# Four edits to a two-layer diffusion step on one core: weight splits held back at sublayer boundaries, modulation of a block on one engine, four-block high and low tiles, and more modulation blocks on TensorE

## Chip, cores and metric

One core of a Trainium2 chip. The metric is device time in microseconds of one execution, as the median of several runs. Beside it stands one execution that was taken with the profiler; all rows below are from that one.

## What is computed

Two layers of a backbone (D = 2048) over 256 tokens: 128 context tokens and 128 noisy ones (below: two groups of 128). Each layer has a mixing and a channel sublayer, each with a norm and a modulation ahead and a norm and a gate behind:

```
def _layer(x, cvec, p, attend):
    shift1, scale1, gate1, shift2, scale2, gate2 = _modulation(cvec, p['w_mod'], p['b_mod'])
    h = _rmsnorm(x, p['g_pre_mix']) * (1 + scale1) + shift1
    au, av, q, k, v, ga, gb = jnp.split(h @ p['w_in'], SPLITS, axis=-1)
    ya = _spatial_gating(au, av, p['sgu_ln_g'], p['sgu_ln_b'], p['sgu_w'], p['sgu_b'])
    yb, extra = attend(_heads(q), _heads(k), _heads(v))
    merged = jax.nn.sigmoid(ga) * (ya @ p['w_pa']) + jax.nn.sigmoid(gb) * (_merge_heads(yb) @ p['w_pb'])
    x = x + gate1 * _rmsnorm(merged @ p['w_out'], p['g_post_mix'])
    h = _rmsnorm(x, p['g_pre_ffn']) * (1 + scale2) + shift2
    f = jnp.square(jax.nn.relu(h @ p['w_ff1'])) @ p['w_ff2']
    x = x + gate2 * _rmsnorm(f, p['g_post_ffn'])
    return x, extra
```

`_modulation` is `silu(cvec) @ w_mod + b_mod` with a 2048 x 12288 matrix per layer and one vector per group of tokens. All weights are float32.

## The kernel before, in words

**Products.** A weight comes in tiles of 128x1024 float32 (512 KB), 928 of them; a tile is a *job* (class `Job`, L51), and eight jobs with the same outputs are a *column* of 512 outputs. `split` (L297) cuts a raw tile into a high and a low part: ACT copies it rounded (`wh`), DVE subtracts (`wl`). Activations stand as high and low parts too, in tiles for two blocks of 128 rows (`pair`, four blocks in the change). `mm_half` (L304) issues for each job and group of tokens high x high, low x high and high x low (L318 to L320 with tokens as output rows, L327 to L329 with features as rows).

**Order.** The body writes a list `items` of jobs and calls, and a loop (L1046 to L1087) goes through it once; the order of the program's text is the order on each engine. Before each item `advance` (L1009) issues what may run ahead: loads of modulation blocks (`mraw`) and of raw tiles (`raw`), through `fetch` (L1004) on SP's queue, and splits while fewer than `P["cap"]` split tiles wait for use.

**Modulation.** The two modulation matrices are 48 *quads* of eight blocks of 512 KB. `MOD_ON_PE` (L45), made from `PE_QUADS` (L38), says where a quad runs: on DVE by `mod_dot` (L180), two SCALAR_TENSOR_TENSOR per block, or on PE by `mod_mm` (L225, matmuls at L234), closed for a quad by `mod_fin` (L209, transposes at L216). Between jobs the loop puts in a block when a pace allows it; for DVE only if its load is under a limit, for PE two at a time. `need(n)` (L859) is the due time: it runs blocks until n quads are done, whatever they wait for. `ENDS` (L37) holds n for the four sublayers' ends.

**A boundary.** At a sublayer's end, x gets the gated, normed output, is normed again, scaled and shifted, and turned so that it can be the next product's stationary side. This is `chain` (L760), one for each group: the norm's factor, four updates of x on DVE and four Squares on ACT, the second norm's factor, and then for each of four tiles of 512 columns the scaling (DVE, tile `s`), four transposes on PE (L803), the modulation (even blocks DVE, odd blocks ACT), the high copy (ACT) and the low subtraction (DVE). PE's cover for it are two columns that `lay_halves` (L839) lays out by halves: the last column of the old sublayer first for group 0, then for group 1, then the first column of the next in the same way; a half job is six matmuls. `step` pumps the chain of group 0 from the middle of the last column on, that of group 1 from the middle of the next, at the positions of `CHAIN_AT`. `cap(HELD)`, eight items ahead of the last column, lets eight splits be made ahead. There are three such boundaries (mixing to channel, channel to the second layer's mixing, mixing to channel), and one end without a next column. At the second one x is also spilled to HBM (L778).

```
        first = (lambda a: lambda p: (lambda: step(0, p - 8, *a)()))(args)
        lay_halves(seq[-1], first)
...
                step(0, p + 8, *a)()
                step(1, p, *a)()
...
        lay_halves(seqs[i][0][0], second)
```

All functions that the edits touch:

Of the kernel before, what the change touches and what calls it, by code (L numbers as in the profile page):

```python
# [23 lines left out]
HELD = 8  # L24
# [12 lines left out]
ENDS = [20, 34, 44, 48]  # L37
PE_QUADS = set(range(11)) | {18, 19}  # L38
# [8 lines left out]
CHAIN_AT = (0, 1, 3, 4, 5, 6, 7, 8, 9, 10, 11, 12)  # L47
# [41 lines left out]
def body(tc, io):  # L89
# [153 lines left out]
    def pair():  # L243
        return u4(F32R).rearrange("p (k h t) -> p k h t", k=2, h=2)

    def hi_lo(t, hl):
        act(hl[:, :, 0, :], t, AF.Copy)
        tt(hl[:, :, 1, :], t, f(hl[:, :, 0, :]), op=OP.subtract)
# [22 lines left out]
    def h_part(todo, tiles, r2, l, ma, mb, c, steps, flush):  # L271
        def finish():
            t, hl, s, u = todo.pop(0)
            tt(hl[:, u, 1, :], t[:, s, :], f(hl[:, u, 0, :]), op=OP.subtract)

        t, hls = tiles
        for b0, n in steps:
# [26 lines left out]
    def mm_half(job, gs=(0, 1)):  # L304
# [5 lines left out]
        for j in range(2):  # L310
            kt = 2 * job.kh + j
            hl = G.rhs[kt // 2][:, kt % 2]
            first, last = kt % n == 0, kt % n == n - 1
            if G.tok:
                for g in gs:
                    o = G.ps[:, 512 * g:512 * g + 512]
                    hh, lo = (hl[:, h, 128 * g:128 * g + 128] for h in range(2))
# [3 lines left out]
            else:  # L321
                hh, lo = hl[:, 0, :], hl[:, 1, :]
# [11 lines left out]
    def mixing(l, hs):  # L334
# [31 lines left out]
        def sgu():  # L366
# [22 lines left out]
            ya = [pair() for _ in range(4)]  # L389
            for k in range(4):  # L390
# [21 lines left out]
        S["yav"] = []  # L412
        S["ybv"] = []
# [51 lines left out]
        def attention():  # L465
            yb = [pair() for _ in range(4)]
            for t in range(4):
# [50 lines left out]
                hi, lo = yb[t][:, :, 0, 128:], yb[t][:, :, 1, 128:]  # L518
# [3 lines left out]
            for t in range(2):  # L522
# [79 lines left out]
        def merge(t, ma):  # L602
# [3 lines left out]
            for e in range(2):  # L606
# [5 lines left out]
                hl = pair()  # L612
                act(hl[:, :, 0, :], v4(o, 2), AF.Copy, scale=0.5)
                yield
                yield
                dve.scalar_tensor_tensor(hl[:, :, 1, :], v4(o, 2), 0.5, f(hl[:, :, 0, :]), op0=OP.mult, op1=OP.subtract)
                mg.append(hl)

        def merged(n):
            def go():  # L620
                while len(mg) < n:
                    pump(bg)
            return go
# [69 lines left out]
    def out_stats(Y, src, o, g):  # L693
        act(dump, src, AF.Square, accum_out=Y["st"][g][:, o:o + 1])
        y = Y["y"][o][:, g, :]
        tt(y, src, y, op=OP.mult)

    def ffn(l, hs):
# [4 lines left out]
        def post_ff1(hid):  # L703
            def post(ps):
# [3 lines left out]
                for h in range(2):  # L708
                    hid.append(pair())
                    hi_lo(v4(t)[:, 2 * h:2 * h + 2, :], hid[-1])  # L710
            return post

        def post_ff1_rows(hid):
            def turn(t, g):
# [4 lines left out]
                w = slice(128 * g, 128 * g + 128)  # L719
                for e in range(2):  # L720
                    act(hid[e][:, :, 0, w], v4(o)[:, 2 * e:2 * e + 2, :], AF.Copy)
                yield
                for e in range(2):
                    tt(hid[e][:, :, 1, w], v4(o)[:, 2 * e:2 * e + 2, :], f(hid[e][:, :, 0, w]), op=OP.subtract)

            def post(ps, gs):
                for g in gs:
                    if g == 0:
                        hid.extend([pair(), pair()])
# [451 lines left out]
```

## Time and profile before

| | |
|---|---|
| median of 3 runs | 2870.31 us (2866.93 to 2874.01) |
| profiled execution | 2869.48 us, span 2867.7 us |
| mean granted clock of PE in it | 0.988 |
| busy: PE, PEld, DVE, ACT | 96%, 83%, 74%, 45% of the span |
| HBM | 713.42 MB read, 6.37 MB written, 251 GB/s over the span |

PE is TensorE's matmuls, PEld its weight loads (beside the matmuls), DVE VectorE, ACT ScalarE, SP SyncE, which issues the loads. The busy share is a mean over the whole span. A wait is the idle time ahead of an instruction together with what ended it. The granted clock is a share of full speed. The profiled execution is 0.8 us below the median.

### The profile page before, as it was taken

The numbers are of one execution on the slowest core, as the hardware profiler recorded it, in microseconds if no ns is written. First come the engines' busy times: TensorE is split into PE (matmuls) and PEld (weight loads), VectorE is DVE, ScalarE is ACT, GpSimd is POOL, SyncE is SP. The second block draws the span as 40 slices with busy tenths as digits, with TensorE's granted clock in tenths as the row PEclk, the third lists the DMA queues.
The fourth block names the chain that finished last, engine by engine and source line by source line (L and its number), as shares of the span: only waits on it lengthen the run. The fifth ranks groups of instructions, "written<-read, shape, count | busy, mean of one in ns | idle before, by whom it ended". The sixth has DMA issues, their size and how long they took to land.

```text
span 2867.7 us, 41916 instructions
## 1 busy us (share of the span) xinstructions
PE 2761.1 (96%) x16366; PEld 2386.6 (83%) x16366; DVE 2114.4 (74%) x2782; ACT 1288.7 (45%) x1654; POOL 0.7 (0%) x6
## 2 busy tenths in 40 slices
PE   7999999997799999999989999999979999999998
PEld 5788778884698989989868997888869899898997
DVE  4665878885579898898866888888865555656555
ACT  4344555442544444444454445544445444444443
POOL 0000000000000000000000000000000000000000
PEclk9999999998999999999999999999999999999999
DMA  9978867787468778787856677677845665756653
GB/s 383 363 261 311 288 227 270 264 314 274 148 232 297 271 270 302 258 302 273 299 183 252 234 261 264 238 273 270 312 145 206 206 223 195 249 191 213 218 201 140
DMA packets 204823, 722.57 MB, mean 252 GB/s; under 512 B 22992, under 2 KB 25680, under 8 KB 204624
## 3 DMA queue, kind: packets, MB, share of 16 engines
q1 hardware_dynamic: 204624, 719.89, 70.3%
q8 instruction: 128, 2.10, 0.3%
q14 instruction: 71, 0.58, 0.1%
HBM read 713.42 MB, written 6.37 MB: 251 GB/s over the span
## 4 chain that ended last, share of the span: by engine, by line
PE 91%; DVE 3%; ACT 3%; DMA 1%; issue 1%; SPq 0%; DVEq 0%; ACTq 0%
PE mm L318 18%; PE mm L320 18%; PE mm L319 18%; PE mm L327 11%; PE mm L328 11%; PE mm L329 11%; PE aux L234 2%; ACT wh L76 1%; DVE u L76 1%; DVE wl L76 1%; DMA mraw<-wm 1%; DVE s L76 1%; ACT s L76 1%; ACT u L76 1%; PE aux L803 0%
## 5 line engine op out<-in xcount | busy, mean ns | idle before, releaser
L76 DVE TENSOR_TENSOR wl<-raw,wh 128x1024 fp32r<-128x1024 f32 x928 | 1108.0, 1221 | 352.9 <-ACT wh L76 338.9
L76 ACT ACTIVATE wh<-raw 128x1024 fp32r<-128x1024 f32 x928 | 948.7, 1055 | 617.1 <-PE mm L320 175.7
L318 PE MATMUL mm<-wh,u 128*128 128x512 f32 x2368 | 940.9, 397 | 13.6 <-ACT u L76 5.6
L320 PE MATMUL mm<-wh,u 128*128 128x512 f32 x2368 | 929.4, 392 | 1.5 <-DVE u L76 1.5
L319 PE MATMUL mm<-wl,u 128*128 128x512 f32 x2368 | 930.0, 393 | 0.4 <-DVE wl L76 0.4
L327 PE MATMUL mm<-u,wh 128*128 128x256 f32 x2688 | 763.8, 284 | 0.0
L329 PE MATMUL mm<-u,wl 128*128 128x256 f32 x2688 | 761.1, 283 | 0.0
L328 PE MATMUL mm<-u,wh 128*128 128x256 f32 x2688 | 761.1, 283 | 0.0
L318 PEld LDWEIGHTS mm<-wh,u 128*128 128x128 f32 x2368 | 449.7, 190 | 119.5 <-issue 7.7
L320 PEld LDWEIGHTS mm<-wh,u 128*128 128x128 f32 x2368 | 449.2, 190 | 98.1 <-DVE u L76 2.9
L327 PEld LDWEIGHTS mm<-u,wh 128*128 128x128 f32 x2688 | 516.1, 192 | 13.8 <-issue 10.9
L319 PEld LDWEIGHTS mm<-wl,u 128*128 128x128 f32 x2368 | 449.6, 190 | 90.8 <-DVE wl L76 0.8
L328 PEld LDWEIGHTS mm<-u,wh 128*128 128x128 f32 x2688 | 516.1, 192 | 0.4
L329 PEld LDWEIGHTS mm<-u,wl 128*128 128x128 f32 x2688 | 516.1, 192 | 0.0
L76 DVE SCALAR_TENSOR_TENSOR mraw<-mraw,sbc 128x1024 f32<-128x1024 f32 x280 | 343.0, 1225 | 9.7
L76 DVE SCALAR_TENSOR_TENSOR junk<-mraw,sbc 128x1024 bf16<-128x1024 f32 x280 | 340.9, 1217 | 0.0
L76 ACT ACTIVATE u<-mm 128x1024 f32<-128x1024 f32 (+1 forms) x83 | 76.6, 933 | 437.4 <-PE mm L329 273.7
L76 DVE TENSOR_TENSOR u<-u,u 128x512 fp32r<-128x512 f32 (+3 forms) x104 | 75.5, 750 | 184.9 <-ACT u L76 184.2
L76 DVE TENSOR_TENSOR u<-u,mm 128x1024 f32<-128x1024 f32 (+1 forms) x60 | 64.5, 1076 | 90.1 <-PE mm L320 53.7
L76 ACT ACTIVATE u<-u 128x512 fp32r<-128x512 f32 (+3 forms) x116 | 84.2, 753 | 33.2 <-DVE u L76 27.3
L234 PE MATMUL aux<-mraw,csw 128*32 128x512 f32 (+1 forms) x480 | 68.8, 596 | 30.5 <-DMA mraw<-wm 30.4
L76 ACT ACTIVATE u<-aux 128x256 fp32r<-128x256 f32 (+2 forms) x56 | 24.1, 445 | 132.7 <-PE aux L611 60.7
(96 smaller groups left out, 667.5 us busy)
## 6 DMA issues: line engine op xcount, KB each, us to landing
raw<-f SPq DMA_DIRECT2D x512, 512.0 KB, 3.9
mraw<-wm SPq DMA_DIRECT2D x384, 512.0 KB, 4.9
raw<-wi SPq DMA_DIRECT2D x288, 512.0 KB, 4.4
raw<-wo SPq DMA_DIRECT2D x64, 512.0 KB, 7.8
raw<-pa SPq DMA_DIRECT2D x32, 512.0 KB, 4.3
raw<-pb SPq DMA_DIRECT2D x32, 512.0 KB, 4.0
u<-gd SPq DMA_DIRECT2D x32, 256.0 KB, 5.6
u<-xT SPq DMA_DIRECT2D x4, 512.0 KB, 5.8
```

Source lines behind the costliest of these rows:

```text
L76: return fn(out, *a, **k)
L234: nc.tensor.matmul(p[32 * c:32 * c + 32, :128 * nb], csw[:, kt, :], r[:, kt - k0, :], start=kt < 4, stop=kt > 11, skip_group_check=True, t ...
L318: nc.tensor.matmul(o, hh, wh[:, j, :], start=first, stop=False)
L319: nc.tensor.matmul(o, hh, wl[:, j, :], start=False, stop=False)
L320: nc.tensor.matmul(o, lo, wh[:, j, :], start=False, stop=last)
L327: nc.tensor.matmul(o, wh[:, j, s], hh, start=first and b % 2 == 0, stop=False, **kw)
L328: nc.tensor.matmul(o, wh[:, j, s], lo, start=False, stop=False, **kw)
L329: nc.tensor.matmul(o, wl[:, j, s], hh, start=False, stop=last, **kw)
```

## The change

Four things. **Splits at a boundary**: `cap` becomes `held`, which lets ten splits be made ahead rather than eight and holds three raw tiles at most; `ahead(p)` sets the limit item by item: no split in the second half of the last column, one at each of six jobs of the next column's first half, and three at the end of its second half. In the chain the scaling of a tile is put one step ahead (`scaled`). **Modulation of a tile** goes to one engine: an even tile is two TENSOR_TENSOR of 128x512 on DVE with the modulation vector repeated along the tokens, an odd one four ACTIVATE on ACT; one high copy and one low subtraction follow for four blocks. **High and low tiles** hold four blocks each (`quad` for `pair`) everywhere, so that copies and subtractions of two become one; `out_stats` does the Squares of both groups ahead of the products. **PE_QUADS** has 17 quads instead of 13 (12, 14, 16, 38 and 42 added, 19 taken out, 18 kept); `ENDS[1]` is 33 instead of 34, and modulation loads stop at the sublayer's end.

```diff
-HELD = 8
+HELD = 10
+RAW_HELD = 3
...
-ENDS = [20, 34, 44, 48]
-PE_QUADS = set(range(11)) | {18, 19}
+ENDS = [20, 33, 44, 48]
+PE_QUADS = set(range(11)) | {12, 14, 16, 18, 38, 42}
...
-CHAIN_AT = (0, 1, 3, 4, 5, 6, 7, 8, 9, 10, 11, 12)
+CHAIN_AT = (0, 1, 3, 4, 6, 7, 9, 11, 12)
+AHEAD = [0] * 9 + [1, 2, 3, 4, 5, 6] + [6] * 6 + [7, 8, 9]
...
-    def pair():
-        return u4(F32R).rearrange("p (k h t) -> p k h t", k=2, h=2)
+    def quad():
+        return v4(u4(F32R)), v4(u4(F32R))
...
-    def out_stats(Y, src, o, g):
-        act(dump, src, AF.Square, accum_out=Y["st"][g][:, o:o + 1])
-        y = Y["y"][o][:, g, :]
-        tt(y, src, y, op=OP.mult)
+    def out_stats(Y, src, o, gs):
+        src = v4(src, 2)
+        for g in gs:
+            act(dump, src[:, g, :], AF.Square, accum_out=Y["st"][g][:, o:o + 1])
+        for g in gs[::-1]:
+            y = Y["y"][o][:, g, :]
+            tt(y, src[:, g, :], y, op=OP.mult)
...
-                for h in range(2):
-                    hid.append(pair())
-                    hi_lo(v4(t)[:, 2 * h:2 * h + 2, :], hid[-1])
+                hid.append(quad())
+                hi, lo = hid[-1]
+                act(hi, v4(t), AF.Copy)
+                tt(lo, v4(t), f(hi), op=OP.subtract)
...
+        def scaled(o):
+            if o < 4:
+                xr[o] = s2()
+                dve.tensor_scalar(xr[o], X[o][:, g, :], r2, None, op0=OP.mult)
+
+        scaled(0)
+        yield
+        last = None
         for o in range(4):
-            xr = s2()
-            dve.tensor_scalar(xr, X[o][:, g, :], r2, None, op0=OP.mult)
-            if t is not None:
-                low(o - 1, t)
+            if g == 0:
+                hs.append(quad())
+            scaled(o + 1)
+            ps = aux()
+            x = xr.pop(o)
+            for b in range(4):
+                nc.tensor.transpose(ps[:, 128 * b:128 * b + 128], x[:, 128 * b:128 * b + 128], ident)
+            if last is not None:
+                tt(*last, op=OP.subtract)
+            t, ps = v4(s2()), v4(ps)
+            if o % 2 == 0:
+                for m, src, op in ((ma, ps, OP.mult), (mb, t, OP.add)):
+                    mat(ln, m, 4 * o, g), mat(ln, m, 4 * o + 3, g)
+                    tt(t, src, mv[:, ln, m, 4 * o:4 * o + 4, g:g + 1].to_broadcast([128, 4, 128]), op=op)
+            else:
+                for b in range(4):
+                    act(t[:, b, :], ps[:, b, :], AF.Identity, scale=mat(ln, ma, 4 * o + b, g),
+                        bias=mat(ln, mb, 4 * o + b, g))
+            hi, lo = (h[:, :, w] for h in hs[o])
+            act(hi, t, AF.Copy)
+            last = lo, t, f(hi)
             yield
...
-    def cap(n):
+    def held(on):
         def go():
-            P["cap"] = n
+            P["held"], P["cap"] = on, HELD if on else SPLIT_BUFS
         return go
+    def ahead(p):
+        P["cap"] = HELD - max(0, p if p < 8 else 8 if p < 16 else p - 8) + AHEAD[p]
...
-        first = (lambda a: lambda p: (lambda: step(0, p - 8, *a)()))(args)
+        def first(p, a=args):
+            def go():
+                if p >= 8:
+                    step(0, p - 8, *a)()
+                    ahead(p - 8)
+            return go
...
                 step(1, p, *a)()
+                ahead(p + 8)
...
-            if P["nm"] < len(mloads) and P["mlive"] < MOD_BUFS + (START_BUFS if P["nm"] < 64 else 0):
+            if P["nm"] < min(len(mloads), P["end"]) and P["mlive"] < MOD_BUFS + (START_BUFS if P["nm"] < 64 else 0):
...
-            if P["nl"] < len(loads) and P["live"] < RAW_BUFS - (P["cap"] == HELD) * 2 and loads[P["nl"]].after <= P["nm"]:
+            if P["nl"] < len(loads) and P["live"] < (RAW_HELD if P["held"] else RAW_BUFS) and loads[P["nl"]].after <= P["nm"]:
```

Lines shift a little: the tokens' matmuls L318 to L320 become L316 to L318, the modulation's L234 becomes L236 and L216 becomes L218, the recording helper L76 becomes L78.

**PE at the first boundary**, where the first half of the last column begins (`u_...` is an activation tile, `mm` the column's PSUM tile). Before:

```order
L320 MATMUL mm<-wh,u_5430 128x512
L234 MATMUL aux<-mraw,csw 32x512 x32
L216 MATMUL aux<-ident,s_5965 128x128 x4
L216 MATMUL aux<-ident,s_5975 128x128 x4
L318 MATMUL mm<-wh,u_4584 128x512
```

Now:

```order
L316 MATMUL mm<-wh,u_5478 128x512
L317 MATMUL mm<-wl,u_5478 128x512
L318 MATMUL mm<-wh,u_5479 128x512
L316 MATMUL mm<-wh,u_4638 128x512
L317 MATMUL mm<-wl,u_4638 128x512
L318 MATMUL mm<-wh,u_4639 128x512
```

The 32 modulation matmuls of quads 18 and 19 (16 blocks, two each) no longer stand between the two columns; the blocks that `need(20)` still forces there are two, on DVE. On PE quads 12, 14, 16 and 18 now stand in fours between jobs of earlier columns.

**DVE at the third boundary**, from the second norm's factor of group 0 on (`s_...<-u_...,tiny` is the scaling that L803's transposes read, `s<-aux,mv` the modulation, `u<-s,u` the low subtraction). Before:

```order
L76 TENSOR_TENSOR wl<-raw,wh 128x1024 x2
L76 TENSOR_REDUCE tiny<-tiny 128x1
L76 RECIPROCAL tiny<-tiny 128x1
L76 TENSOR_TENSOR wl<-raw,wh 128x1024
L76 TENSOR_SCALAR s_18530<-u_18050,tiny 128x512
L76 TENSOR_TENSOR wl<-raw,wh 128x1024
L76 TENSOR_SCALAR s_18551<-aux,mv 128x128 x2
L76 TENSOR_TENSOR wl<-raw,wh 128x1024
L76 TENSOR_SCALAR s_18570<-u_18052,tiny 128x512
```

Now, up to the first splits that are let out:

```order
L78 TENSOR_SCALAR s_18523<-u_17999,tiny 128x512
L78 TENSOR_TENSOR u_18486<-s_18495,u_18485 128x4x128
L78 TENSOR_TENSOR s_18531<-aux,mv 128x512
L78 TENSOR_TENSOR s_18531<-s_18531,mv 128x512
L78 SCALAR_TENSOR_TENSOR u_17993<-u_17789,tiny,u_17993 128x512
L78 SCALAR_TENSOR_TENSOR u_17995<-u_17792,tiny,u_17995 128x512
L78 SCALAR_TENSOR_TENSOR u_17997<-u_17795,tiny,u_17997 128x512
L78 SCALAR_TENSOR_TENSOR u_17999<-u_17798,tiny,u_17999 128x512
L78 TENSOR_TENSOR wl<-raw,wh 128x1024 x2
```

Before, five of the `wl` splits stand among the first group's norm, scaling and modulation. Now none does: they come behind the last tile of the first group's chain and the second group's four updates.

## Rows read from the trace of the kernel before

**Rows 1.** The page's first part: busy time of each engine, its share of the span, and its instructions.

```profile
PE 2761.1 (96%) x16366; PEld 2386.6 (83%) x16366; DVE 2114.4 (74%) x2782; ACT 1288.7 (45%) x1654; POOL 0.7 (0%) x6
```

**Rows 2.** Busy time by stretch of the run (columns: the stretch, its length, then busy us and instructions of PE, PEld, DVE, ACT and POOL, the granted clock of PE, the DMA share, GB/s).

```profile
500.00:600.00 100.00, 100.00 (x454) 82.83 (x453) 87.36 (x111) 39.91 (x43) 0.00 (x0) 1.00 0.75 263
600.00:700.00 100.00, 83.20 (x353) 57.23 (x351) 81.50 (x113) 34.51 (x45) 0.00 (x0) 0.91 0.87 325
...
2100.00:2200.00 100.00, 81.39 (x489) 71.05 (x488) 60.35 (x100) 54.01 (x96) 0.00 (x0) 0.93 0.46 158
```

**Rows 3.** Waits of PE over the whole run: who waits for whom; us in total, times, the longest.

```profile
PE aux L803 <- DVE s L76: 45.1, 17, 4.7
PE aux L234 <- DMA mraw<-wm: 30.4, 16, 12.6
```

**Rows 4.** Timeline of the first boundary's start (start, duration, engine, line, operation, count, idle time before and what ended it); SPq is SP's queue of DMA issues.

```profile
666.73 0.39 PE L320 MATMUL mm<-wh,u 128*128 128x512 f32 x1
...
667.68 34.55 SPq L1007 DMA_DIRECT2D mraw<-wm  x23
...
679.67 1.92 PE L234 MATMUL aux<-mraw,csw 128*32 128x512 f32 x4 [12.55 <-DMA mraw<-wm]
...
705.53 0.48 PE L318 MATMUL mm<-wh,u 128*128 128x512 f32 x1
```

**Rows 5.** Timeline of PE in the first 100 us, where a pair of modulation blocks stands between matmuls of a job.

```profile
93.21 0.39 PE L320 MATMUL mm<-wh,u 128*128 128x512 f32 x1
93.53 1.06 PE L234 MATMUL aux<-mraw,csw 128*32 128x512 f32 x8
...
94.87 0.39 PE L319 MATMUL mm<-wl,u 128*128 128x512 f32 x1
```

**Rows 6.** Timeline of PE in the third boundary, around a group of transposes without a wait.

```profile
2140.34 0.60 PE L803 MATMUL aux<-ident,s 128*128 128x128 f32 x4
...
2141.01 0.40 PE L319 MATMUL mm<-wl,u 128*128 128x512 f32 x1
```

**Rows 7.** Waits of PE in the third boundary (2090 to 2164 us).

```profile
PE aux L803 <- DVE s L76: 13.9, 5, 4.2
PE mm L318 <- ACT s L76: 1.6, 1, 1.6
PE mm L318 <- DVE tiny L76: 1.6, 1, 1.6
PE mm L320 <- DVE u L76: 1.5, 1, 1.5
```

**Rows 8.** Timeline of PE in the third boundary: its first matmul, a wait and matmuls after it, and its end.

```profile
2090.32 0.39 PE L318 MATMUL mm<-wh,u 128*128 128x512 f32 x1
...
2114.22 1.11 PE L803 MATMUL aux<-ident,s 128*128 128x128 f32 x4 [4.20 <-DVE s L76]
...
2115.99 0.63 PE L320 MATMUL mm<-wh,u 128*128 128x512 f32 x1
2116.42 0.63 PE L318 MATMUL mm<-wh,u 128*128 128x512 f32 x1
...
2162.13 0.39 PE L318 MATMUL mm<-wh,u 128*128 128x512 f32 x1
...
2163.49 0.28 PE L327 MATMUL mm<-u,wh 128*128 128x256 f32 x1
```

**Rows 9.** Timeline of PE: the first boundary's end, the second one's start and end (the first one's start is in rows 4).

```profile
778.74 0.28 PE L327 MATMUL mm<-u,wh 128*128 128x256 f32 x1
...
1452.47 0.39 PE L318 MATMUL mm<-wh,u 128*128 128x512 f32 x1
...
1529.23 0.39 PE L318 MATMUL mm<-wh,u 128*128 128x512 f32 x1
```

**Rows 10.** Timeline of DVE in the third boundary.

```profile
2111.09 0.15 DVE L76 TENSOR_REDUCE tiny<-tiny 128x1 f32<-128x4 f32 x1
2111.60 0.16 DVE L76 RECIPROCAL tiny<-tiny 128x1 f32<-128x1 f32 x1 [0.36 <-ACT tiny L76]
2112.55 1.23 DVE L76 TENSOR_TENSOR wl<-raw,wh 128x1024 fp32r<-128x1024 f32 x1 [0.78 <-ACT wh L76]
2113.69 0.48 DVE L76 TENSOR_SCALAR s<-u,tiny 128x512 f32<-128x512 f32 x1
```

**Rows 11.** Groups of instructions by line, engine, operation and shape in 2090 to 2175 us (count, then busy us, the mean ns of one, idle time before and its releasers); the last line is from the page's list of DMA issues (count, KB each, us to landing).

```profile
L76 ACT ACTIVATE wh<-raw 128x1024 fp32r<-128x1024 f32 x17 | 17.0, 1046 | 0.0
...
L76 ACT ACTIVATE s<-aux,mv 128x128 f32<-128x128 f32 x16 | 7.3, 458 | 19.6 <-DVE s L76 19.6
L76 DVE TENSOR_SCALAR s<-aux,mv 128x128 f32<-128x128 f32 x16 | 6.5, 409 | 7.8 <-ACT s L76 4.2 <-PE aux L803 3.5
...
L76 DVE SCALAR_TENSOR_TENSOR u<-u,tiny,u 128x512 f32<-128x512 f32 x8 | 5.5, 746 | 0.0
L76 ACT ACTIVATE dump<-u 128x512 bf16<-128x512 f32 x8 | 5.0, 629 | 1.3 <-DVE u L76 1.1
...
L76 DVE TENSOR_TENSOR u<-mm,u 128x512 f32<-128x512 f32 x4 | 2.8, 690 | 6.1 <-ACT dump L76 6.1
...
L76 ACT ACTIVATION_READ_ACCUMULATOR dump<-u 128x1 f32 x8 | 1.5, 187 | 0.0
...
raw<-f SPq DMA_DIRECT2D x512, 512.0 KB, 3.9
```

More of the change, by code (lines that the diff above doesn't have):

```diff
@@ L272, in finish @@
         def finish():
-            t, hl, s, u = todo.pop(0)
-            tt(hl[:, u, 1, :], t[:, s, :], f(hl[:, u, 0, :]), op=OP.subtract)
-        t, hls = tiles
+            t, s = todo.pop(0)
+            tt(low[:, s, :], t[:, s, :], f(high[:, s, :]), op=OP.subtract)
+        t, (high, low) = tiles
         for b0, n in steps:
@@ L316, in mm_half @@
                     o = G.ps[:, 512 * g:512 * g + 512]
-                    hh, lo = (hl[:, h, 128 * g:128 * g + 128] for h in range(2))
+                    hh, lo = (h[:, 128 * g:128 * g + 128] for h in hl)
                     nc.tensor.matmul(o, hh, wh[:, j, :], start=first, stop=False)
@@ L388, in sgu @@
             bs = v4(S["bs"], 8)
-            ya = [pair() for _ in range(4)]
+            ya = [quad() for _ in range(2)]
             for k in range(4):
@@ L465, in attention @@
         def attention():
-            yb = [pair() for _ in range(4)]
+            yb = [quad() for _ in range(2)]
             for t in range(4):
@@ L611, in merge @@
                         nc.tensor.transpose(o[:, T * b + 128 * g:T * b + 128 * g + 128], t[:, c:c + 128], ident)
-                hl = pair()
-                act(hl[:, :, 0, :], v4(o, 2), AF.Copy, scale=0.5)
+                if e == 0:
+                    mg.append(quad())
+                    out = mg[-1]
+                hi, lo = (h[:, 2 * e:2 * e + 2, :] for h in out)
+                act(hi, v4(o, 2), AF.Copy, scale=0.5)
                 yield
                 yield
-                dve.scalar_tensor_tensor(hl[:, :, 1, :], v4(o, 2), 0.5, f(hl[:, :, 0, :]), op0=OP.mult, op1=OP.subtract)
-                mg.append(hl)
+                dve.scalar_tensor_tensor(lo, v4(o, 2), 0.5, f(hi), op0=OP.mult, op1=OP.subtract)
+                S["mg"] += 1
         def merged(n):
             def go():
-                while len(mg) < n:
+                while S["mg"] < n:
                     pump(bg)
@@ L728, in post @@
                     if g == 0:
-                        hid.extend([pair(), pair()])
+                        hid.append(quad())
                     t = s2()
@@ L817, in body @@
+        tt(*last, op=OP.subtract)
     modi = [0]
@@ L914, in go @@
             if steps[0][0] == 0:
-                start["t"] = X[c], [pair(), pair()]
-                hs[0].extend(start["t"][1])
+                start["t"] = X[c], quad()
+                hs[0].append(start["t"][1])
             if P["cap"] == 0:
```

72 lines of the change are left out of this document (21 added, 51 removed).

## Prediction, on record before the changed kernel ran

> **What bounds the kernel now.** First the page: PE is busy for 96% of the span [rows 1]. A mean of 96% over stages can hide where the missing 4% lies, so next the stretches of 100 us: between boundaries PE is at 100.00 of 100 us, while the stretches with a boundary in them show 83.20 and 81.39 [rows 2]. Third the waits of PE over the whole run: two rows carry nearly all, 45.1 us in the transposes of the boundary chain (L803), which wait for DVE's scaled `s` tile, and 30.4 us in the modulation matmuls (L234), which wait for their blocks from HBM [rows 3]. So there are two rules for pricing an edit. Outside the boundaries and the start, everything that PE gets is paid in full, and everything that DVE or ACT loses is worth nothing. At a boundary PE waits, and the order of DVE and ACT sets the time.
>
> The first boundary has a stall of its own. Its timeline [rows 4]: PE's last matmul of the half starts at 666.73, SP then issues 23 modulation loads over 34.55 us, PE's first L234 comes at 679.67 after 12.55 us of waiting, and the next matmul of a weight job at 705.53. From 666.96 (666.73 and a pitch of 0.23) that is **38.6 us** without a weight matmul. The listing before shows all 32 matmuls of quads 18 and 19 together there. `need(20)` forces them, each block waiting for its own load, since only a few buffers are free.
>
> The boundaries proper run from the first matmul of a sublayer's last column to the first one after the next sublayer's first column. The third takes 2163.49 - 2090.32 = 73.2 us [rows 8]; the first 778.74 - 705.53 = 73.2 and the second 1529.23 - 1452.47 = 76.8 [rows 4, 9]. PE's own work in one is 192 matmuls and 8 groups of transposes. Six matmuls took 2163.49 - 2162.13 = 1.36 us, 0.2267 each [rows 8]; a group of transposes costs 2141.01 - 2140.34 = 0.67 less one matmul, 0.44 [rows 6]. That is 43.5 + 3.5 = 47.0, so a boundary loses 26.2, 29.8 and 26.2 us. Of the third one's loss, 18.6 us stand as waits [rows 7]; the rest is matmuls 0.43 apart after a wait [rows 8].
>
> Why PE waits there: a weight split stands on DVE ahead of what PE wants (the `wl` of 1.23 us at 2112.55 directly ahead of the `s` at 2113.69 [rows 10], eight held splits in a boundary), and the modulation of a tile changes engine block by block, DVE 0.41, ACT 0.46, DVE, ACT [rows 11], each waiting for the other because they write one tile.
>
> **The change, part by part.**
>
> *The stall.* With quads 12, 14 and 16 on PE as well, the planner, which runs PE blocks in pairs without asking for DVE's load, is further ahead when `need(20)` comes: in the change's listing no L236 stands ahead of the last column's halves. What is still forced is two blocks, both on DVE. Gain: the whole 38.6.
>
> *More blocks on PE.* Six quads (12, 14, 16, 18, 38, 42) now run on PE between jobs, where PE is full; 18 and 19 ran inside the stall. A pair of blocks (x8 matmuls) takes 94.87 - 93.21 = 1.66 us less two matmuls, 1.20 [rows 5]; a quad has four pairs and one group of transposes, 4 x 1.20 + 0.44 = 5.24. Six quads: **+31.4 us**. The 32 blocks that DVE loses are worth nothing there, since PE waits for DVE at no place outside the boundaries. If PE were not full (83 to 100 in the stretch), part of the 31.4 would be hidden. Lower bound 25, only the busy 1.06 of a pair counted; above, the measured 1.20 leaves little room, and I keep 31.4.
>
> *The boundaries.* No split is let out during the second half of the last column, so DVE and ACT do the chain alone; two more splits are made ahead (10), six are let out one a job in the next column, and the chain scales a tile one step ahead. What PE still waits for, from the change's listing with the durations of rows:
> - The longest: after the last matmul of the last column come the second group's Square and read-out (0.63 + 0.19), the product 0.69, the small steps from reduce to reciprocal (2111.76 - 2111.09 = 0.67) [rows 10, 11], then on DVE the first chain's scaling 0.48 and three operations of the size of the 0.69, one update of 0.75, then on ACT four Squares with read-outs (4 x 0.82) and only then the `wh` of the first split let out, 1.05. The sum is 9.8 us. PE has two jobs and a group of transposes in that time, 12 x 0.2267 + 0.44 = 3.2. A wait of about 7, with hand-offs taken as 7.9.
> - Splits let out one by one: `wh` 1.05 and `wl` 1.22 make 2.27 a split against 1.36 of PE for a half job, six times 0.9 = 5.5.
> - ACT's four blocks of an odd tile stand ahead of a `wh`: 4 x 0.46 = 1.8.
> - The switch between halves, 1.8, about as the 1.6 and 1.5 of before [rows 7], and some 1.5 at the end.
>
> Together 18.5 a boundary, where 26.2, 29.8 and 26.2 were lost: a gain of 7.7 + 11.3 + 7.7 = 26.7. One operation has no row: the product of a PSUM tile of 128x512 with a vector repeated along it, two of these for every even tile in place of blocks. The nearest rows are the product of a PSUM tile and an SBUF tile of the same size, 0.69, and a block by a scalar, 0.41 [rows 11]; above stands the 1.22 of twice the elements. I take 0.69, the same shape. Eight of them lie in a boundary, about half of them in PE's path: 0.41 would give back some 3 us over all boundaries, 1.22 would cost some 6 and at most 13. I take off 2 more for matmuls at the lower clock after the new long waits. **-25 us.**
>
> [...]
>
> *Wider tiles.* High and low tiles of four blocks instead of two mean fewer, longer instructions on ACT and DVE in the feed-forward columns, the gating and the attention. They lie beside PE at 100% [rows 2] and are worth 0; without that cover they would be a gain. The same holds for the squares of both groups ahead of the products.
>
> *Loads.* Held raw tiles go from four to three, and modulation loads stop at the sublayer's end. On SP nothing new is issued; 21 blocks more have to come in before the first boundary, 11 MB, where 500 to 600 us shows a DMA share of 0.75 at 263 GB/s [rows 2], so a quarter is free: 88 GB/s, 125 us of some 500. Price 0.
>
> **Sum:** 2869.5 (the profiled execution; the median of the runs shown is 0.8 above) - 38.6 + 31.4 - 25 = **2837 us**.
>
> **The rivals.**
> [...]
> - *The boundaries gain nothing.* The waits for splits let out take the place of the waits for the chain in full: 2869.5 - 38.6 + 31.4 = 2862. For it: 2.27 us for a split against 1.36 for a half job. Against: only six are let out, and 26 us were lost by eight. 7%.
> - *The stall only moves.* The added loads come late, and PE waits for blocks between jobs in the 500 us ahead of the boundary; with about 30 of the 38.6 given back 2867. For it: DMA at 0.87 in 600 to 700 [rows 2]. Against: blocks are used only when they are some jobs old, and 0.75 before that. This is also the case in which the change doesn't do what it says. 4%.
> - *Slower: the let-out splits wait for their raw tiles.* With three held raw tiles the fourth split's load is issued only when one is freed, and a raw tile takes 3.9 us from issue to landing [rows 11] against 1.36 for a half job: up to 2.5 us for each of 18 splits, 46. These waits stand in place of the chain's, so the gain of 25 goes too: 2862 + 46 = 2908. It decides from 0.9 us a split on, (2878 - 2862) / 18. For it: at the second boundary the spilling of x stands ahead on the same queue. Against: all loads go out as soon as a split has read its tile, and the first three are there. 6%, since probably only some of the 18 would be late.
>
> **How the numbers follow.** Forecast 72%, the rivals 11, 7, 4 and 6. About 0.3%, 8.6 us, is what a measurement of this kernel can tell from no change, so faster means below 2861. The forecast and the clock's case lie there: 83%. Without gain at the boundaries or with the stall moved: within, 11%. Slower 6%. The range: below, the new product at 0.41 (3), the pairs at 25 (6), no clock loss (2) and hand-offs at the sum's 7 instead of 7.9 (3): 2823, and 2819 with the waits for splits half hidden; above, the clock's case with the product at 1.22 throughout, 2846 + 13 = 2859. I give 2819 to 2859; outside lie the last three rivals, 17%.
>
> **What would show it.** Right: no wait of L236 for `mraw` near 667 us, a first boundary without a gap; the stretches 500 to 700 at 100% with 16 L236 groups more; each boundary 64 to 67 us from its first matmul to the column after; the longest wait in it 7 to 9 us at the third job of the next column, released by ACT's `wh` or the `wl` behind it. Wrong: splits of a next column that wait for `raw`, with matmuls behind them (the slower rival), boundaries at 73 us, pairs at another price than 1.20, or a wait of L236 for its load ahead of the boundary.

## The result, and the profile after

The changed kernel took **2851.08 us** as the median of 4 runs (2849.79 to 2852.58), the kernel before 2870.46 beside it: a ratio of 0.9933, 95% interval 0.9915 to 0.995. That is 19.4 us less, where 33 were forecast; the time lies in the stated range, 2819 to 2859. The profiled execution has a span of 2848.0 us against 2867.7.

The page's first part, after; it answers to [rows 1]:

```profile
PE 2772.1 (97%) x16510; PEld 2385.9 (84%) x16510; DVE 2030.6 (71%) x2568; ACT 1285.3 (45%) x1596; POOL 0.7 (0%) x6
```

PE has 11 us more work, DVE 84 us less. The next view cuts the run at the same matmuls in both kernels: from the first weight matmul to the first matmul of the last mixing column, then boundary, stretch, boundary, stretch, boundary, and the rest (columns as in [rows 2]):

```profile
28.13:691.67 663.54, 657.61 (x3786) 518.21 (x3786) 452.05 (x575) 297.64 (x407) 0.00 (x0) 0.99 0.82 300
691.67:761.93 70.26, 56.54 (x230) 43.89 (x228) 42.95 (x70) 32.93 (x66) 0.00 (x0) 0.85 0.39 140
761.93:1434.54 672.61, 672.61 (x4326) 616.42 (x4325) 571.57 (x730) 307.56 (x307) 0.00 (x0) 1.00 0.76 271
1434.54:1502.02 67.48, 54.28 (x225) 42.27 (x224) 37.51 (x58) 31.85 (x64) 0.00 (x0) 0.90 0.50 184
1502.02:2076.48 574.46, 570.96 (x3227) 484.73 (x3225) 467.36 (x613) 264.10 (x356) 0.00 (x0) 1.00 0.76 270
2076.48:2144.23 67.75, 54.50 (x229) 42.13 (x228) 38.02 (x62) 32.94 (x66) 0.00 (x0) 0.90 0.39 137
2144.23:2839.46 695.23, 694.45 (x4422) 634.18 (x4420) 406.22 (x430) 307.35 (x313) 0.00 (x0) 1.00 0.60 207
```

The same cuts in all kernels of this text, in us. The two stretches left out, between the first and second boundary and behind the third, took 672.6 to 673.7 and 695.2 to 696.0 in every kernel.

| kernel | median us | first stretch | 1st boundary | 2nd boundary | stretch between 2nd and 3rd | 3rd boundary |
|---|---|---|---|---|---|---|
| before | 2870.5 | 677.2 | 73.2 | 76.8 | 561.1 | 73.2 |
| the change | 2851.1 | 663.5 | 70.3 | 67.5 | 574.5 | 67.8 |
| e1_quads_only | 2862.9 | 660.7 | 73.3 | 76.5 | 571.8 | 73.1 |
| e3_dve_38_42 | 2840.5 | 662.5 | 69.4 | 67.6 | 563.3 | 70.7 |
| e4_three_ahead | 2838.5 | 664.9 | 63.7 | 65.8 | 573.4 | 63.7 |
| e5_not_held | 2843.8 | 663.3 | 65.4 | 68.3 | 574.6 | 65.4 |
| e6_by_blocks | 2874.2 | 666.1 | 76.1 | 76.3 | 573.7 | 75.7 |
| e7_two_quads | 2853.8 | 677.3 | 70.3 | 67.5 | 563.3 | 69.4 |
| e8_fill | 2847.0 | 666.1 | 69.9 | 64.9 | 573.1 | 67.3 |
| e9_spread | 2828.8 | 662.8 | 59.9 | 62.5 | 574.2 | 61.5 |
| e10_spread_dve | 2817.8 | 663.1 | 60.4 | 62.8 | 563.3 | 60.1 |
| e11_three_quads | 2809.8 | 657.5 | 60.5 | 61.5 | 563.3 | 61.5 |

The kernel before took 2868.6, 2868.0 and 2868.8 us beside e1 to e5, e6 to e9, and e10 and e11; the ratios below are to those. The change itself was measured beside 2870.5, so a difference of its median to those of other kernels is read to 2 us at best. The lengths are of one profiled execution each. The change and the seven edits of it that keep its quads in the first stretch take 662.5 to 666.1 us there, so differences of 3 us in that column are not read.

So of the 19.7 us of span, 13.6 come from the first stretch, 17.7 from the boundaries (3.0, 9.3 and 5.4), 1.5 from the two stretches left out, and 13.4 are lost between the second and the third boundary.

Waits of PE over the whole run, after, against [rows 3]:

```profile
PE mm L316 <- ACT wh L78: 27.8, 9, 6.7
PE aux L236 <- DMA mraw<-wm: 15.6, 5, 12.4
```

L803, 45.1 us before, is gone from the list: the chain's transposes wait no more. In its place the matmuls of a job wait for ACT's `wh`. The 15.6 us of L236 are 12.4 at the kernel's start, which stand in the trace of before as 12.55 too, and 2.55 at 631 us.

Waits of PE in the third boundary after, 13.3 us against the 18.6 of [rows 7]:

```profile
PE mm L316 <- ACT wh L78: 9.0, 3, 6.7
PE mm L317 <- DVE wl L78: 2.0, 3, 0.8
PE mm L316 <- DVE tiny L78: 1.6, 1, 1.6
PE mm L316 <- ACT s L78: 0.7, 1, 0.7
```

PE's timeline there (answers to [rows 8]):

```profile
2104.04 0.39 PE L318 MATMUL mm<-wh,u 128*128 128x512 f32 x1
2111.12 0.79 PE L316 MATMUL mm<-wh,u 128*128 128x512 f32 x1 [6.69 <-ACT wh L78]
2112.38 0.80 PE L317 MATMUL mm<-wl,u 128*128 128x512 f32 x1 [0.46 <-DVE wl L78]
2112.97 0.63 PE L318 MATMUL mm<-wh,u 128*128 128x512 f32 x1
2113.40 0.63 PE L316 MATMUL mm<-wh,u 128*128 128x512 f32 x1
...
2117.67 0.41 PE L318 MATMUL mm<-wh,u 128*128 128x512 f32 x1
```

and ACT's at the same place, where the `wh` stands behind the last of four Squares:

```profile
2107.14 0.63 ACT L78 ACTIVATE dump<-u 128x512 bf16<-128x512 f32 x1
...
2109.40 0.63 ACT L78 ACTIVATE dump<-u 128x512 bf16<-128x512 f32 x1
2109.94 0.19 ACT L78 ACTIVATION_READ_ACCUMULATOR dump<-u 128x1 f32 x1
2110.03 1.99 ACT L78 ACTIVATE wh<-raw 128x1024 fp32r<-128x1024 f32 x2
```

The wait that the prediction put at the third job, 7.9 us, is there with 6.69, behind the Squares as worked out. What was not worked out follows it: from 2112.97 on the matmuls come 0.43 apart, for about 4 us (2117.67 is the last). The modulation with the vector repeated along the tokens takes what was taken for it, 0.69 (DVE, after):

```profile
2098.04 0.69 DVE L78 TENSOR_TENSOR s<-aux,mv 128x512 f32<-128x512 f32 x1 [2.13 <-PE aux L803]
2098.77 0.69 DVE L78 TENSOR_TENSOR s<-s,mv 128x512 f32<-128x512 f32 x1
```

### The profile page after: what moved, and what is told of

Its sections match the earlier page's. It is cut to its first block, busy times and chain, and to the rows that moved or that the text cites. A ratio compares the mean times of both kernels' runs of the same rounds, so it can differ in the third digit from the quotient of the medians.

```text
span 2848.0 us, 41915 instructions
## 1 busy us (share of the span) xinstructions
PE 2772.1 (97%) x16510; PEld 2385.9 (84%) x16510; DVE 2030.6 (71%) x2568; ACT 1285.3 (45%) x1596; POOL 0.7 (0%) x6
## 3 DMA queue, kind: packets, MB, share of 16 engines
q1 hardware_dynamic: 204624, 719.89, 70.7%
## 4 chain that ended last, share of the span: by engine, by line
PE 94%; ACT 2%; DVE 2%; DMA 1%; issue 0%; SPq 0%; DVEq 0%; ACTq 0%
PE mm L316 19%; PE mm L317 18%; PE mm L318 18%; PE mm L325 11%; PE mm L326 11%; PE mm L327 11%; PE aux L236 2%; DMA mraw<-wm 1%; DVE wl L78 1%; ACT u L78 1%; ACT wh L78 1%; ACT s L78 1%; DVE u L78 0%; ACT dump L78 0%; DVE s L78 0%
## 5 line engine op out<-in xcount | busy, mean ns | idle before, releaser
L78 DVE TENSOR_TENSOR wl<-raw,wh 128x1024 fp32r<-128x1024 f32 x928 | 1108.0, 1221 | 373.9 <-ACT wh L78 355.4
L78 ACT ACTIVATE wh<-raw 128x1024 fp32r<-128x1024 f32 x928 | 949.1, 1055 | 651.5 <-PE mm L317 150.1
L316 PE MATMUL mm<-wh,u 128*128 128x512 f32 x2368 | 942.4, 398 | 37.8 <-ACT wh L78 27.8
L318 PE MATMUL mm<-wh,u 128*128 128x512 f32 x2368 | 928.5, 392 | 2.4 <-DVE u L78 2.4
L316 PEld LDWEIGHTS mm<-wh,u 128*128 128x128 f32 x2368 | 448.4, 189 | 158.9 <-ACT wh L78 37.9
L318 PEld LDWEIGHTS mm<-wh,u 128*128 128x128 f32 x2368 | 448.2, 189 | 98.8 <-DVE u L78 3.8
L325 PEld LDWEIGHTS mm<-u,wh 128*128 128x128 f32 x2688 | 515.8, 192 | 13.8 <-issue 10.5
L78 DVE SCALAR_TENSOR_TENSOR mraw<-mraw,sbc 128x1024 f32<-128x1024 f32 x248 | 303.8, 1225 | 8.8
L78 DVE SCALAR_TENSOR_TENSOR junk<-mraw,sbc 128x1024 bf16<-128x1024 f32 x248 | 301.9, 1217 | 8.3 <-DMA mraw<-wm 8.3
L78 ACT ACTIVATE u<-mm 128x1024 f32<-128x1024 f32 (+1 forms) x83 | 76.6, 933 | 429.7 <-PE mm L327 277.9
L78 DVE TENSOR_TENSOR u<-u,u 128x1024 fp32r<-128x1024 f32 (+4 forms) x74 | 72.9, 992 | 207.4 <-ACT u L78 206.9
L78 DVE TENSOR_TENSOR u<-u,mm 128x1024 f32<-128x1024 f32 (+1 forms) x60 | 64.1, 1076 | 103.4 <-PE mm L318 67.1
L78 ACT ACTIVATE u<-u 128x1024 f32<-128x1024 f32 (+3 forms) x86 | 81.4, 949 | 32.4 <-DVE u L78 27.2
L236 PE MATMUL aux<-mraw,csw 128*32 128x512 f32 (+1 forms) x608 | 76.0, 585 | 15.7 <-DMA mraw<-wm 15.6
L78 ACT ACTIVATE u<-aux 128x512 fp32r<-128x512 f32 (+2 forms) x48 | 23.6, 492 | 114.4 <-PE aux L607 68.7
```

Source lines behind the costliest of these rows:

```text
L78: return fn(out, *a, **k)
L236: nc.tensor.matmul(p[32 * c:32 * c + 32, :128 * nb], csw[:, kt, :], r[:, kt - k0, :], start=kt < 4, stop=kt > 11, skip_group_check=True, t ...
L316: nc.tensor.matmul(o, hh, wh[:, j, :], start=first, stop=False)
L318: nc.tensor.matmul(o, lo, wh[:, j, :], start=False, stop=last)
L325: nc.tensor.matmul(o, wh[:, j, s], hh, start=first and b % 2 == 0, stop=False, **kw)
```

## The experiments

**e1_quads_only**: the table alone, on the kernel before.

```diff
-ENDS = [20, 34, 44, 48]
-PE_QUADS = set(range(11)) | {18, 19}
+ENDS = [20, 33, 44, 48]
+PE_QUADS = set(range(11)) | {12, 14, 16, 18, 38, 42}
```

> The kernel before with the changed table of quads on PE and the changed ENDS alone; boundaries, chain and tiles as before. My theory, from the traces of before and after, is that this part gives about nothing: the stall of 38.6 us at the first boundary goes, but the stretch from the first weight matmul to the first boundary gets only 13 to 14 us shorter and the one between the second and third boundary 13 us longer (two quads at 5.24, and waits that they bring). So 2870 us, within 4 of before, and the boundaries 73, 77 and 73 us as before. Rival, the sum of the prediction (- 38.6 + 31.4): 2863 us. Rival two, that the quads also help the boundaries by taking work off DVE: boundaries at 70 us or less and 2860 or below.

Measured 2862.9 against 2868.6, ratio 0.9982 (0.9973 to 0.999): 5.7 us less, near the prediction's sum of 7.2, and not the nothing that I had read off the change's trace. The first stretch lost 16.5 us, the one with quads 38 and 42 got 10.7 longer, 10.7 / 2 = 5.4 a quad. No wait of L234 stands at the boundary, and the boundaries are as they were, so the quads don't help them.

**e3_dve_38_42**: the change with two quads fewer on PE.

```diff
-PE_QUADS = set(range(11)) | {12, 14, 16, 18, 38, 42}
+PE_QUADS = set(range(11)) | {12, 14, 16, 18}
-MOD_LIMIT = [2.0, 2.0, 2.0, 2.0]
+MOD_LIMIT = [2.0, 2.0, 3.0, 2.0]
```

> The changed kernel with quads 38 and 42 back on DVE, and the planner's limit of DVE load for that sublayer at 3.0 rather than 2.0, so that they are done in time. My theory: PE is full there, so the stretch between the second and the third boundary gets back the 13 us that it lost: two quads at 5.24 and the two waits at 2026 and 2030 us. 2838 us, the stretch at 561 to 563 us. Rival: DVE (70 to 88% busy there) has no room for 16 blocks of 2.44 us, 39 us in all; its splits come late and PE waits for them instead, 2848 to 2855 us with new waits for wl.

Measured 2840.5, ratio 0.99 (0.9885 to 0.9915). The stretch is 563.3: 11.2 us come back, and DVE has room for the 16 blocks. The third boundary took 2.9 us more, which I have not explained; with the same quads e10_spread_dve, below, has nothing of it (60.1, against 61.5 in e9_spread). Of the 13.4 us that the change loses here, 10.5 are the two quads' work. The rest goes with two waits of PE for DVE, 1.71 us at 2026 us and 0.68 at 2030, that this run doesn't have (it has two others, 1.60 at 1605 us and 0.96 at 1802). At the first of them, in the change (DVE, then PE):

```profile
2022.12 1.23 DVE L78 SCALAR_TENSOR_TENSOR junk<-mraw,sbc 128x1024 bf16<-128x1024 f32 x1 [7.67 <-DMA mraw<-wm]
...
2025.68 0.68 DVE L78 SCALAR_TENSOR_TENSOR u<-aux,u 128x512 fp32r<-128x512 f32 x1
```

```profile
2026.41 0.50 PE L318 MATMUL mm<-wh,u 128*128 128x512 f32 x1 [1.71 <-DVE u L78]
```

DVE stands 7.67 us in front of a modulation block whose load hasn't landed; behind it in the queue is a low tile that PE needs, and PE waits 1.71 us. The late block held up what was queued behind it on DVE.

**e5_not_held**: the change with the splits at boundaries let out as before.

```diff
-HELD = 10
-RAW_HELD = 3
+HELD = 8
+RAW_HELD = 4
...
     def ahead(p):
-        P["cap"] = HELD - max(0, p if p < 8 else 8 if p < 16 else p - 8) + AHEAD[p]
+        pass
```

> The changed kernel with the splits handled at boundaries as before: eight ahead, four raw tiles, and a new split whenever one is used up, also in the second half of the last column; the chain, the modulation on one engine, the tiles and the quads as in the change. My theory: keeping splits off DVE and ACT during the chain is what made the boundaries shorter, so they go back to 71 to 77 us, with L803 waiting for DVE again, and the time to 2864 to 2869 us. Rival: the modulation on one engine and the scaling one step ahead did it; boundaries stay at 68 to 70 us and the time at 2851 to 2855.

Measured **2843.8**, ratio 0.9914 (0.9901 to 0.9928): not 15 us slower than the change but 7 us faster (5 by the ratios), and below the rival's 2851 to 2855 too. My theory fell. Holding the splits back is not where the boundaries' gain came from; as the change does it, it costs. The boundaries (columns as in [rows 2]) and PE's waits in the third:

```profile
691.53:756.88 65.35, 51.51 (x225) 39.53 (x224) 42.29 (x66) 37.68 (x71) 0.00 (x0) 0.97 0.40 138
1429.92:1498.21 68.29, 54.16 (x225) 41.92 (x224) 42.14 (x63) 37.53 (x70) 0.00 (x0) 0.93 0.46 164
2072.80:2138.15 65.35, 50.90 (x225) 39.61 (x224) 39.24 (x60) 37.68 (x71) 0.00 (x0) 0.97 0.38 131
```

```profile
PE mm L318 <- DVE u L78: 7.1, 4, 2.7
PE aux L803 <- DVE s L78: 4.3, 2, 2.9
PE mm L316 <- DVE tiny L78: 1.6, 1, 1.6
PE mm L316 <- ACT s L78: 1.5, 1, 1.5
```

The waits are 14.5 us, more than the change's 13.3; the longest is 2.9 instead of 6.7, and the granted clock 0.97 instead of 0.90. What got shorter is the slow matmuls: counted as under e8_fill below, they cost 3.1 us here and 6.1 in the change.

**e6_by_blocks**: e5_not_held with the modulation in turns again.

```diff
-            if o % 2 == 0:
-                for m, src, op in ((ma, ps, OP.mult), (mb, t, OP.add)):
...
+            for b in range(4):
+                sc, sh = mat(ln, ma, 4 * o + b, g), mat(ln, mb, 4 * o + b, g)
+                if b % 2 == 0:
+                    dve.tensor_scalar(t[:, b, :], ps[:, b, :], sc, sh, op0=OP.mult, op1=OP.add)
+                else:
+                    act(t[:, b, :], ps[:, b, :], AF.Identity, scale=sc, bias=sh)
```

> The kernel e5_not_held (2843.8 us, boundaries 65.4, 68.3 and 65.4) with the modulation of a tile block by block on DVE and ACT in turns, as before; the scaling one step ahead, the tiles of four blocks and the quads stay as in the change. My theory now: not the holding, but the modulation on one engine made the boundaries shorter; with turns they go back to 72 to 76 us each and the time to 2864 to 2870. Rival: the scaling one step ahead did it, since DVE's s was what L803 waited for; boundaries stay at 65 to 69 us and the time within 5 us of 2844.

Measured 2874.2, ratio 1.0018 (1.0009 to 1.0027): the whole gain of the boundaries is gone, and a little more. Its third boundary, DVE and then ACT:

```profile
2119.80 0.41 DVE L78 TENSOR_SCALAR s<-aux,mv 128x128 f32<-128x128 f32 x1
2120.73 0.41 DVE L78 TENSOR_SCALAR s<-aux,mv 128x128 f32<-128x128 f32 x1 [0.53 <-ACT s L78]
2123.28 1.22 DVE L78 TENSOR_TENSOR wl<-raw,wh 128x1024 fp32r<-128x1024 f32 x1 [2.13 <-ACT wh L78]
...
2125.42 0.41 DVE L78 TENSOR_SCALAR s<-aux,mv 128x128 f32<-128x128 f32 x1
```

```profile
2120.24 0.46 ACT L78 ACTIVATE s<-aux,mv 128x128 f32<-128x128 f32 x1 [2.78 <-DVE s L78]
...
2122.20 1.04 ACT L78 ACTIVATE wh<-raw 128x1024 fp32r<-128x1024 f32 x1
```

This is a ring. ACT's block, the second of the tile, waits 2.78 us for DVE's first; the `wh` stands behind it on ACT; DVE's next `wl` waits 2.13 us for that `wh`; and DVE's next tile stands behind the `wl`. One tile with one split takes 2125.42 - 2119.80 = 5.6 us, though neither engine works more than 3.2 us of it. The kernel before has the same ring in its third boundary (DVE, then ACT):

```profile
2118.81 1.22 DVE L76 TENSOR_TENSOR wl<-raw,wh 128x1024 fp32r<-128x1024 f32 x1 [2.08 <-ACT wh L76]
```

```profile
2122.59 0.46 ACT L76 ACTIVATE s<-aux,mv 128x128 f32<-128x128 f32 x1 [2.86 <-DVE s L76]
```

In that boundary ACT's blocks wait 21.4 us in all for DVE's here, 19.6 in the kernel before, and not at all in e5_not_held, where the high copy's wait for DVE's whole tile is left (13.9 us, 4 times). With a tile on one engine the hand-over falls to one in two tiles. Not run: the modulation on one engine without the scaling one step ahead and the four-block tiles, and turns with the splits held back.

**e8_fill**: the change with 24 matmuls more at the long wait, whose result nobody reads.

```diff
                 ahead(p + 8)
+                if p == 2:
+                    j = seqs[k][0][0][1]
+                    o = aux()
+                    for _ in range(24):
+                        nc.tensor.matmul(o, j.group.rhs[0][0][:, 0, 0:128], j.parts[0][:, 0, :], start=True, stop=True)
```

> The changed kernel with 24 more matmuls on PE in each of the three boundaries, between the second and the third half job of the next column, where PE waits 6.1 to 6.7 us; they write a PSUM tile that nobody reads, 24 x 0.2267 = 5.4 us of work. It measures what the clock costs by itself. Theory: a large part of what was forecast and not gained is matmuls at the lower clock, 6.1 to 8.0 us in each boundary, that follow the long wait; with the wait filled the clock stays up, boundaries get 3 to 5 us shorter in spite of the added work, 64 to 66 us, and the time is 2837 to 2843 us. Rival: the chain sets the end anyway, and the slow matmuls lie in time in which PE would wait; boundaries stay at 67 to 70 us and the time within 3 us of 2851. Rival two: the added work comes on top, 2855 us and more.

Measured 2847.0, ratio 0.9922 (0.9909 to 0.9934); by the intervals that is not clear of the change, so the boundaries have to show the effect (same columns):

```profile
694.07:763.92 69.85, 61.17 (x253) 47.97 (x252) 42.92 (x70) 32.94 (x66) 0.00 (x0) 0.90 0.40 140
1436.54:1501.44 64.90, 56.56 (x250) 44.50 (x248) 37.51 (x58) 31.85 (x64) 0.00 (x0) 0.97 0.52 192
2074.49:2141.78 67.29, 58.35 (x253) 45.92 (x252) 37.77 (x62) 32.94 (x66) 0.00 (x0) 0.95 0.39 138
```

With 5.4 us more of work each the boundaries are 0.4, 2.6 and 0.5 us shorter, the clock 0.90, 0.97 and 0.95 where it was 0.85, 0.90 and 0.90. So the clock does set part of the time. Matmuls and transposes that come more than 0.33 after the one ahead, a wait between them taken off, cost 20.4 us in the change's three boundaries (90 of them, each counted less 0.2267), and 14.9 here (73 without the added ones). Some of that is not the clock: 21 of the 90 stand directly behind a wait; without those it is 14.6 and 10.7. The size was below what I had expected, 64 to 66 us a boundary and 2837 to 2843 in all: the other waits, of up to 2 us, stay, and so do slow matmuls. In the first boundary the clock is 0.90 and they still cost about 7 us, beside 8.7 us in which PE is idle (69.85 - 61.17).

**e4_three_ahead** and **e9_spread**: the change with splits let out earlier.

```diff
-AHEAD = [0] * 9 + [1, 2, 3, 4, 5, 6] + [6] * 6 + [7, 8, 9]
+AHEAD = [0] * 8 + [3, 4, 5] + [6] * 10 + [7, 8, 9]                        # e4_three_ahead
+AHEAD = [0] * 4 + [2] * 4 + [2, 3, 4, 5, 6, 6] + [6] * 7 + [7, 8, 9]      # e9_spread
```

> The changed kernel with three splits let out at the start of the next column's first half, ahead of the second group's updates and Squares, and then one a job: AHEAD is [0] * 8 + [3, 4, 5] + [6] * 10 + [7, 8, 9]. My theory is that the longest wait of a boundary, 6.1 to 6.7 us, is the first let-out split standing behind the second group's four Squares on ACT, and that the second group's chain has slack, since no L803 waits in the changed kernel: the wait goes down to 2 us, another of 3 to 5 us comes at the fourth let-out split, boundaries get 5 to 7 us shorter, 61 to 63 us, and the time is 2831 to 2836 us. Rival: the second group's chain is what ends last; put back by three splits (3.7 us of DVE) it makes L803 wait in the second half, and the time stays within 4 us of 2851.

> The changed kernel with two splits let out in the second half of the last column, at the point at which ACT and DVE wait for the first tile's transposes, and the others one a job from the next column's first job on: AHEAD is [0] * 4 + [2] * 4 + [2, 3, 4, 5, 6, 6] + [6] * 7 + [7, 8, 9]. Theory: the boundary is bound by the order on ACT and DVE, and splits cost least where both are idle; the wait behind the four Squares goes, the others are under 3 us, the clock falls less: boundaries 61 to 63 us and 2830 to 2835 us, faster than e4_three_ahead (2838.5). Rival: splits in the last column's second half put back the first group's chain as in e5_not_held; boundaries 65 us or more and 2843 us or more.

Measured 2838.5 (ratio 0.9896, 0.9882 to 0.9909) and **2828.8** (0.9861, 0.9847 to 0.9874). Both beat the change. e4_three_ahead fell somewhat short of its expectation, with boundaries of 63.7, 65.8 and 63.7: no L803 waits, but low tiles of the first group stand behind its three `wl` on DVE (3.49 us at 2097 us in the third boundary, in which PE waits 7.0 us for low tiles). e9_spread went past its own, with 59.9, 62.5 and 61.5. Its waits in the third:

```profile
PE mm L316 <- ACT wh L78: 3.0, 1, 3.0
PE mm L316 <- ACT s L78: 1.8, 1, 1.8
PE mm L316 <- DVE tiny L78: 1.6, 1, 1.6
PE mm L318 <- DVE u L78: 1.4, 2, 0.9
PE mm L317 <- DVE wl L78: 0.5, 1, 0.5
```

8.3 us in all against 13.3, the longest 3.0. The granted clock of this boundary:

```profile
2060.41:2121.92 61.51, 53.33 (x230) 41.90 (x229) 38.38 (x62) 32.82 (x66) 0.00 (x0) 0.92 0.41 149
```

Two splits in the gap in which ACT and DVE wait for the first tile's transposes cost the chain nothing that shows.

**e7_two_quads**, **e10_spread_dve**, **e11_three_quads**: fewer quads on PE; the last two with e9_spread's AHEAD.

```diff
+PE_QUADS = set(range(11)) | {14, 18}            # e7_two_quads
+MOD_LIMIT = [6.0, 2.0, 3.0, 2.0]
...
+PE_QUADS = set(range(11)) | {12, 14, 16, 18}    # e10_spread_dve
+MOD_LIMIT = [2.0, 2.0, 3.0, 2.0]
...
+PE_QUADS = set(range(11)) | {14, 16, 18}        # e11_three_quads
+MOD_LIMIT = [3.0, 2.0, 3.0, 2.0]
```

> The changed kernel with quads 14 and 18 alone on PE behind the first eleven (12, 16, 38 and 42 on DVE), and the planner's limit of DVE load at 6.0 in the first sublayer and 3.0 in the third, so that DVE has them done in time. Theory: PE is full outside the boundaries, so each quad taken off PE gives back 5.24 us and the waits that it brought: beside the 10 us that e3_dve_38_42 gave, another 10 to 13 ahead of the first boundary; 2828 to 2831 us, the stretch from the first weight matmul to the first boundary at 650 to 653 us. Rival: with DVE over 85% busy there its splits come late; the stretch stays at 660 to 664 us with waits for wl, and the time at 2840 or more.

> Both edits that gained by themselves: the splits spread as in e9_spread and quads 38 and 42 on DVE as in e3_dve_38_42. Theory: the two lie in different stretches, so they add up: 2828.8 less 10 to 11 is 2818 us; boundaries 60 to 63 us, the stretch between the second and the third at 563 us. Rival: the third boundary pays for it, since more modulation blocks are still on DVE ahead of it (it took 70.7 us in e3_dve_38_42, 67.8 in the changed kernel): 2821 to 2824 us.

> e10_spread_dve with quad 12 on DVE too, and the limit of DVE load in the first sublayer at 3.0 (6.0 in e7_two_quads, where the background steps of attention, which the loop puts off while DVE's load is over 5, came late and PE waited 17.7 us for them). Theory: at 3.0 these steps are not put off, PE gives up one quad of 5.24 us and nothing comes late: the stretch from the first weight matmul to the first boundary 656 to 659 us and 2812 to 2815 us in all. Rival: DVE has no room for it next to attention; PE waits there as in e7_two_quads, and the time is 2818 us or more.

e7_two_quads missed: 2853.8 (0.9949, 0.9937 to 0.9962). The first stretch went up by 14 us, but by another wait than the rival's. PE's waits in 400 to 600 us:

```profile
PE aux L548 <- DVE u L78: 10.6, 2, 5.3
PE aux L501 <- ACT u L78: 7.4, 2, 7.1
```

These are attention's transposes, not splits. The limit of 6.0 lets DVE's planned load stand above 5, over which the loop puts the background steps of attention off; they then come all at once, and from 400 to 600 us PE is busy for 181.6 of 200 us, at a granted clock of 0.94, where the change has 199.5 and 1.00. e11_three_quads, with 3.0 (and one quad more on PE), has no wait of L548. e10_spread_dve took 2817.8 (0.982, 0.9806 to 0.9833), the two gains added up; e11_three_quads **2809.8** (0.9793, 0.978 to 0.9806), with the limit at 3.0 and one quad less than e10_spread_dve: 59 us under the kernel before, and the fastest of all kernels here.

## Why the prediction was right, and where not

*The stall* (-38.6): gone, as forecast. *The quads' price*: 5.24 holds; 24 pairs in the change that stand between matmuls of 512 columns take 1.198 each, as forecast. Quads and stall together were to give -7.2 and gave -5.7 when run alone. In the change they gave about nothing (-13.6 in the first stretch, +13.4 in the other). Part of that is waits that the forecast had at 0: 2.55 us for a block's load at 631 us, which e1_quads_only has too (2.67), and 1.71 and 0.68 behind the late block on DVE, which it doesn't have. That the change's first stretch is 2.8 us longer than that of e1_quads_only is not explained, and it is of the size that is not read above. The claim that DVE's relief is worth nothing held. The rival of blocks that come late was right in kind, and a small one.

*The boundaries* (-25): -17.7. Two errors partly cancel, and that the sum came near is in part luck. The waits were put too high (18.5 us a boundary; 13.7, 13.2 and 13.3 were measured) and the clock too low: 2 us in all were taken off, and the matmuls that came slowly cost 8.0, 6.3 and 6.1 us in the three, about as much as before (5.9, 9.1 and 6.8). The term that failed is "I take off 2 more for matmuls at the lower clock". No run shows those 2 us for all boundaries together: in the trace of before the ten matmuls behind the one wait of 4.20 us, from 2114.99 to 2118.93, take 3.94 us for nine steps where 0.2267 each makes 2.04, so that wait alone goes with 1.9 us, and the change's three boundaries lost 20.4. The forecast sets 18.5 us of waits against a loss of 26.2 that holds 18.6 of waits and 7.6 of slow matmuls: it takes nothing off the waits, and the whole gain of the third boundary is slow matmuls that were to be gone. Measured, it is the other way round: over the three the waits fell by 16.6 us (19.1, 19.1 and 18.6 before), and the slow matmuls by 1.4. The clock's case, the 11% and the 2846 of the range, was right in place and sign, and short in size: it is 12 us instead of 2, about 2 at each of six long waits (with which the forecast's sum gives 2847, not 2846), where 20.4 were measured. Its argument (each wait pays more than its length) was given 11% because I took slow matmuls to lie in time in which PE would wait anyhow; e8_fill, with 5.4 us more work in each boundary and boundaries 0.4, 2.6 and 0.5 us shorter, shows that not all do. In the change's third boundary the matmuls behind the 6.69 us wait come 0.43 apart (2112.97 to 2113.40), those ahead of it 0.23 (2103.81 to 2104.04).

*The cause of the boundaries' gain* was wrong in the step "no split is let out during the second half of the last column, so DVE and ACT do the chain alone". e5_not_held and e6_by_blocks show that it hangs on the modulation on one engine: without the holding the boundaries are 65.4, 68.3 and 65.4, without the one engine as well 76. I had costed that edit at nothing but its new operation, since it saves ACT and DVE only 0.2 to 0.4 us a tile. The ring through both queues was in [rows 11] as ACT's 19.6 us of idle time ahead of its blocks, and I took only durations and the hand-over within a tile from those rows, not the split between.

*Wider tiles* (0): -1.5 in the stretches that hold most of them; right. *The slower rival*: in the change's three boundaries no engine waits for a raw tile's load; three raw tiles are enough.

Open: how the clock's cost would divide among the single waits. e8_fill fills most of one wait a boundary (in the third the waits for ACT's `wh`, 9.0 us with one of 6.7, become 4.4 with none over 2.0) and leaves seven.

## What to carry to other kernels

When two engines hand pieces of one tile to each other in turns and both also carry a second stream that passes from one to the other, the queues can lock into a ring, as here (21.4 us of ACT's time in the third boundary of e6_by_blocks, none in that of e5_not_held): give a tile to one engine before moving the second stream out of the way. Work held back to clear a path has to come back somewhere: let it out where both engines idle, not all behind the chain's next step; e9_spread did so, and its boundaries are 5 to 10 us shorter than the change's. Before moving work onto the engine that is full, see whether the engine that has room was only kept from it by a limit, as with the two quads that gave 11.2 us back in e3_dve_38_42.

## What the runs showed of the hardware

Long waits and the clock: in the third boundary 13.3 us of waits with one of 6.7 went with a granted clock of 0.90 (the change), and 14.5 us with none over 2.9 with 0.97 (e5_not_held). The longest wait alone doesn't go with the clock, though: e9_spread's third boundary, with 8.3 us of waits and none over 3.0, had 0.92. Nor does the sum of the waits: in e8_fill the first boundary, with PE idle for 8.7 us (69.85 - 61.17), had 0.90, and the third, with 8.9 (67.29 - 58.35), 0.95. What else does is open.

A DVE TENSOR_TENSOR of 128x512 with an operand repeated along the free dimension took 0.690 us as a product with its other operand in PSUM (`s<-aux,mv`) and 0.692 as a sum with it in SBUF (`s<-s,mv`), in the change's third boundary; the product of two full operands of that size (`u<-mm,u`) took 0.686 there.
